# Counting the filling steps of an attention loop from what was really taken, and moving one gate job forward

## The chip, the cores and the metric

The kernel runs on one core of a Trainium2 chip. The core has five engines, each with its own queue of instructions that it works through in order: TensorE (PE; its weight loads are shown as PEld), VectorE (DVE), ScalarE (ACT), GpSimd (POOL) and SyncE (SP, which here only issues transfers). Engines wait for each other through semaphores. The metric is the device time of one execution in microseconds, the median of several runs.

## The reference

One layer of a hybrid encoder on 1024 tokens of width 1024, in float32: a normalised input goes into a wide projection; stick-breaking attention (8 heads of 64) and a gated linear recurrence (4 heads of 128) run on parts of it; their outputs are merged by gates, projected, and followed by a squared-ReLU MLP. Cut to the part around the change:

```python
xn = rmsnorm(x, norm1_g[layer])
u = xn @ w_in[layer].astype(f32)
q_sb, k_sb, v_sb, f_raw, i_hg, q_hg, g_hg, gate_sb, gate_hg = jnp.split(u, list(c), axis=-1)
...
# attention, for each head and each block of 128 queries
z = jnp.einsum('bhqd,bhkd->bhqk', qi, k) * scale
mask = kpos[None, :] < qpos[:, None]
log_beta = jax.nn.log_sigmoid(z)
log_rem = jnp.where(mask, log_beta - z, 0.0)
between = lax.cumsum(log_rem, axis=3, reverse=True) - log_rem
w = jnp.where(mask, jnp.exp(log_beta + between), 0.0)
out = jnp.einsum('bhqk,bhkd->bhqd', w, v)
...
o_hg = merge_heads(o_hg) * jax.nn.silu(g_hg)
merged = g_a * (o_sb @ w_o_sb) + g_b * (o_hg @ w_o_hg)
```

## The kernel before, in words

Every float32 product is made from a high and a low part, so one projection of 128 columns for 512 tokens takes 24 matmuls of 512 columns (`three`, eight times), and two such halves make a job.

Attention runs over 64 items, 8 heads times 8 query blocks, each head's blocks in the order 7, 0, 6, 1, 5, 2, 4, 3. Block b has (b+1)*128 keys. An item passes through four functions. `scores` (line 767) makes the scores `z` on PE and two sigmoids of them on ACT, `rm` and `bt`, and sets one column of `bt` on POOL. `weights` (798) runs the scan over `rm` and multiplies `bt` by it, both on DVE. `turn` (824) transposes `bt` on PE into `pw` and splits that into a high part on ACT (`wTh`) and a low part on DVE (`wTl`). `values` (867) multiplies two finished blocks with V on PE into `po`, and ACT and DVE bring the result into `osb`. The loop at the end of the kernel prepares items ahead: in turn i it calls `weights` for item i+1 and `scores` for item i+2, and then `turn` for item i.

Between these calls it advances a list of other matmul work, `Stream` (487). A job in it is a generator; `step` runs one piece of it, which is six matmuls for a projection. `advance(n, upto)` runs n steps, `finish(upto)` all steps up to a job. The jobs were put in at lines 1458 to 1467: the first job (head 0's queries and keys, and all of V, 45 steps), then queries and keys of heads 1 to 4, then the recurrence's `q_job(0)` and the gate job `raw_job(KT)`, then heads 5 to 7, `f_job(0)`, `f_job(1)`, `q_job(1)`, `f_job(2)`, and `raw_job(KT + 1)`, whose number is `j_att`. A job for queries and keys, f or q has 9 steps, a raw job 8; the last step of each only closes it. `KT` is 8, so the tiles of the two raw jobs are called `wga8`, `pga`, `pgq` and `wga9`: they make the two plain output gates of the recurrence (`g_hg`) together with a partial product that later gates reuse. When a job starts, its weights are split into high and low parts (`wqk2h`, `wqk2l`) and those of the next two jobs are split or loaded, out of a pool with two raw buffers.

The end of a half of a queries-and-keys job (`qk_epilogue`, 664) copies high parts on ACT (`KS`, `QH`), takes low parts on DVE (`KS`, `QL`), and copies Q's two parts into the other 64 partitions by two transfers issued on POOL.

Which order an engine's instructions get is set by the scheduler that builds the kernel, with two lanes for PE: "main" (attention) and "fill" (the stream); a block of filling may not run ahead of the main lane by more than `AHEAD` = 2 blocks.

The loop's budget before:

```python
n_fill = 9 * (NHS - 1 + 5) + 7 + 7 + 4
n_first = 4
...
st.finish(j_qk[items[min(i + 4, len(items) - 1)][0]])
...
want = n_first + (i + 1) * (n_fill - n_first) // len(items)
st.advance(want - done, j_att)
done = want
```

`finish` makes sure that a head's queries and keys are there before its scores. Behind the loop `st.finish(j_att)` runs whatever is left, and the recurrence's stages go on from there.

Of the kernel before, what the change touches and what calls it, by code (L numbers as in the profile page):

```python
# [23 lines left out]
KT = D // P  # L24
# [15 lines left out]
def kernel(  # L40
# [34 lines left out]
    def slot(name, dt=F32):  # L75
        return spool.tile([P, 1024], dt, tag="s", name=name)
# [7 lines left out]
    def bank(name):  # L84
        return psum.tile([P, 512], F32, tag="p", name=name)
# [10 lines left out]
    class Lane:  # L96
        def __init__(self):
            self.ends = []
            self.last = None
            self.gates = ()  # L100
# [9 lines left out]
    def open_block(name):  # L110
        cur[0] = name
        lane = lanes[name]
        lane.gates = (lane.last,)
        if name == "main":
            lane.ends.append(lane.last)
        else:
            ends = lanes["main"].ends
            lane.gates += tuple(ends[-AHEAD : len(ends) - AHEAD + 1])
# [16 lines left out]
    def load(dst, src):  # L135
        last_load[0] = after(nc.sync.dma_start(dst, src), last_load[0])
# [342 lines left out]
    def cols_unit(name, parts):  # L479

        dmas, c = [], 0
        for mat, c0, n in parts:
            dmas.append((c, n, mat[:, c0 : c0 + n].rearrange("(k p) c -> p k c", p=P)))
            c += n
        return Unit(name, [dmas])

    class Stream:
        def __init__(self, eager=False):
            self.eager = eager
            self.jobs = []  # L490
            self.pos = 0
            self.gen = None
            self.steps = 0
            self.owed_t = None

        def add(self, units, body):
            self.jobs.append((units, body))
            return len(self.jobs)
# [25 lines left out]
        def step(self):  # L524

            if self.gen is None:
                if self.pos >= len(self.jobs):
                    return False
                self.steps = 0
                self._start()  # L530
            self.steps += 1
            if self.owed_t and self.steps == 6:
                self.owed_t.split_t(hg_level[0] or turn_lo[0])
                self.owed_t = None
            open_block("fill")
            if next(self.gen, StopIteration) is StopIteration:
                self.gen = None
                self.pos += 1
            return True
# [11 lines left out]
    st = Stream()  # L551

    def three(ps, wh, wl, xh, xl, first, last, goes_on=False):
        matmul(ps, wh, xh, start=first, stop=False, skip_group_check=goes_on)
        matmul(ps, wh, xl, start=False, stop=False, skip_group_check=goes_on)
        matmul(ps, wl, xh, start=False, stop=last, skip_group_check=goes_on)

    def proj_half(ps, hl, mov, nk, half, wcol=lambda k: k * P, ts=slice(0, 512)):
        wh, wl = hl
        for kt in range(nk):  # L560
            c = wcol(kt)
            xh, xl = (t[:, ts] for t in mov(kt, half))
            three(ps, wh[:, c : c + P], wl[:, c : c + P], xh, xl, kt == 0, kt == nk - 1)
            if kt % 2 == 1:
                yield

    def proj_jobs(group, acts):


        def body():  # L570
            for half in range(2):
                for name, unit, ep in group:
                    ps = bank(f"{name}_{half}")
                    yield from proj_half(ps, unit.hl[0], acts.mov, KT, half)
                    ep(ps, half)

        return st.add([u for _, u, _ in group], body)
# [86 lines left out]
    def qk_epilogue(h):  # L664
        def ep(ps, half):
            if half == 0:
                qk[h] = tuple(slot(f"{n}{h}", F32R) for n in ("QH", "QL", "KS"))
            QH, QL, KS = qk[h]
            cs = slice(half * 512, (half + 1) * 512)
            hi_copy(KS[0:64, cs], ps[64:128])  # L670
            hi_copy(QH[0:64, cs], ps[0:64])
            lo_sub(KS[64:128, cs], ps[64:128], KS[0:64, cs])
            last_lo[0] = lo_sub(QL[0:64, cs], ps[0:64], QH[0:64, cs])
            for Q in (QH, QL):
                nc.gpsimd.dma_start(Q[64:128, cs].bitcast(F32), Q[0:64, cs].bitcast(F32))

        return ep

    def qk_item(h):
        u = cols_unit(f"wqk{h}", [(W_IN, C_Q + h * DHS, DHS), (W_IN, C_K + h * DHS, DHS)])  # L680
        return f"pjqk{h}", u, qk_epilogue(h)
# [78 lines left out]
    j_qk = {0: j_first}  # L760

    QB_ORDER = (7, 0, 6, 1, 5, 2, 4, 3)
    items = [(h, qb) for h in range(NHS) for qb in QB_ORDER]
# [472 lines left out]
    def half(name, dt=F32):  # L1236
        return hpool.tile([P, 512], dt, tag="h", name=name)
# [36 lines left out]
    def gate_bias(which, cb):  # L1274
        return prm[:, BG + which * KT + cb : BG + which * KT + cb + 1]
# [44 lines left out]
    def raw_job(cb):  # L1320
        u = raw_units[cb]

        def steps_of(ps, wt, w0, half_, k0, start):
            wh, wl = u.hl[wt]
            for k in range(4):
                c = (w0 + k) * P
                xh, xl = xn.mov(k0 + k, half_)
                three(
                    ps, wh[:, c : c + P], wl[:, c : c + P], xh, xl, start and k == 0, k == 3, True
                )  # L1330
                if k % 2 == 1:
                    yield

        def body():
            p1, p14, g1 = (half(f"{n}_{cb}") for n in ("p1", "p14", "g1"))
            ps, p4 = bank(f"pga{cb}"), bank(f"pgq{cb}")
            if 6 <= cb < KT:
                load_g1(cb - 6)
            if 5 <= cb < KT:
                sb_units[cb - 5].load()  # L1340
            if 3 <= cb < KT - 1:
                osb[cb - 3] = slot(f"osr{cb}")
                load(osb[cb - 3], od[cb - 3])
            yield from steps_of(ps, 0, 0, 0, 0, True)
            hi_behind[0] = nc.scalar.copy(p1, ps)
            nc.scalar.dma_start(pd[cb][:, 0, :], p1)
            u.split_t()
            st.prefetch()
            hi_behind[0] = None
            yield from steps_of(p4, 1, 0, 1, 4, True)  # L1350
            add(p14, p1, p4)
            if cb == 3 or cb == KT - 1:
                whole_input(1, int(cb == KT - 1))
            nc.gpsimd.dma_start(pd[cb][:, 1, :], p14)
            yield from steps_of(ps, 0, 4, 0, 4, False)
            if cb < KT:
                nc.scalar.activation(g1, ps, AF.Sigmoid, bias=gate_bias(0, cb))
            else:
                nc.scalar.activation(g1, ps, AF.Sigmoid)
                mul(g1, ps, g1)  # L1360
            nc.scalar.dma_start(gd[cb], g1)
            if 4 <= cb < KT:
                a_sb.put(cb - 4, osb.pop(cb - 4))

        return st.add([u], body)
# [3 lines left out]
    def load_g1(cb):  # L1369
        g1r[cb] = half(f"g1r{cb}")  # L1370
        load(g1r[cb], gd[cb])
# [4 lines left out]
    def whole_input(i, j):  # L1376
        for kp in range(2):
            h, l = (t.bitcast(F32) for t in xn.t[i, 2 * j + kp])
            nc.gpsimd.dma_start(l, h, accum_op=ALU.add)
            whole[i, j, kp] = l  # L1380
# [76 lines left out]

    for h in range(1, NHS):
        j_qk[h] = proj_jobs([qk_item(h)], xn)
        if h == 4:  # L1460
            q_job(0)
            raw_job(KT)
    f_job(0)
    f_job(1)
    q_job(1)
# [1 line left out]
    j_att = raw_job(KT + 1)  # L1467
# [827 lines left out]
    scores(*items[1])  # L2295

    n_fill = 9 * (NHS - 1 + 5) + 7 + 7 + 4
    n_first = 4
    ready = deque()
    wsums = out_weight_sums()  # L2300
    done = 0
    for i, it in enumerate(items):
        if i + 1 < len(items):
            weights(*items[i + 1])
        if i + 2 < len(items):
            st.finish(j_qk[items[min(i + 4, len(items) - 1)][0]])
            scores(*items[i + 2])
        if i % 2 == 1:
            next(wsums, None)
        want = n_first + (i + 1) * (n_fill - n_first) // len(items)  # L2310
        st.advance(want - done, j_att)
        done = want
        before = ready.popleft() if ready else None

        def between():
            if before:
                values(*before)

        r = turn(*it, between)
        if i == len(items) - 2:  # L2320
            attended[0] = turn_lo[0]
        if it[1] != NT - 1:
            between()
        if r:
            ready.append(r)
# [128 lines left out]
```

## Time and profile before

| | us |
|---|---|
| median of 3 runs | 1438.32 |
| lowest and highest run | 1438.10, 1438.45 |
| profiled execution, its own time | 1437.93 |
| its span from first to last instruction | 1436.2 |
| attention's stretch in it (first 1024-wide scan to last score) | about 60 to 322 |

Times in the trace count from the span's first instruction. A row of the timeline has the start, the duration, the engine, the line, the operation, the output and inputs by the program's tile names, the shape and the count; what stands in brackets behind it is idle time of the engine just before, and what released it. A row of the grouped view has the count, then busy time and the mean in nanoseconds, then idle time ahead of the group. Durations of PE rows overlap, so the distance between two starts tells what a matmul costs in a stream.

### The profile page before, as it was taken

How to read it: one execution, taken by the hardware profiler on the slowest of the kernel's cores; microseconds unless marked ns; L12 is line 12 of the kernel's file. 1: busy time of each engine (PE TensorE's matmuls, PEld its weight loads, DVE VectorE, ACT ScalarE, POOL GpSimd, SP SyncE). 2: the span in 40 equal slices, each digit the busy share in tenths (PEclk: the TensorE clock that was granted, in tenths of full speed). 3: DMA queues.
4: the chain of work that ended last, by engine and by line, in shares of the span. 5: the costliest groups of instructions: out<-in, count | busy, mean ns of one | idle time of the engine just before them, and what ended most of it. 6: DMA issues, size and time to landing. Idle time of an engine off the chain costs nothing.

```text
span 1436.2 us, 19231 instructions
## 1 busy us (share of the span) xinstructions
PE 1423.2 (99%) x7056; PEld 1193.2 (83%) x7056; DVE 1118.6 (78%) x1537; ACT 678.0 (47%) x1177; POOL 146.6 (10%) x338
## 2 busy tenths in 40 slices
PE   9999999999999999999999999999999999999998
PEld 7888888888888888888888888888888888888886
DVE  6579999899677898798788898666666758668765
ACT  6366666664233444333244674444444433524343
POOL 3012222110001031000000300000000000000042
PEclk9999999999999999999999999999999999999999
DMA  7123435434015775545477405444446974776725
GB/s 237 29 66 89 114 88 107 74 82 130 17 45 155 234 190 194 163 160 187 147 272 249 176 30 198 139 138 144 159 154 215 348 268 158 265 275 251 275 101 181
DMA packets 161334, 233.54 MB, mean 163 GB/s; under 512 B 26028, under 2 KB 93144, under 8 KB 161240
## 3 DMA queue, kind: packets, MB, share of 16 engines
q1 hardware_dynamic: 145400, 190.11, 39.3%
q0 software_dynamic: 11520, 34.61, 9.6%
q10 hardware_dynamic: 4320, 7.60, 1.4%
q8 instruction: 55, 0.90, 0.3%
q14 instruction: 39, 0.32, 0.1%
HBM read 167.27 MB, written 65.01 MB: 162 GB/s over the span
## 4 chain that ended last, share of the span: by engine, by line
PE 76%; DVE 0%; POOL 0%; ACT 0%; issue 0%
PE pm L128 21%; PE pX L128 9%; PE pW L128 6%; PE pY L128 6%; PE gX L128 4%; PE gY L128 4%; PE pys L128 3%; PE pga L128 3%; PE pji L128 3%; PE pyh L128 3%; PE sl L128 3%; PE pwX L128 2%; PE pjq L128 2%; PE pgq L128 2%; PE pwY L128 2%; PE pwW L128 2%
## 5 line engine op out<-in xcount | busy, mean ns | idle before, releaser
L156 ACT CAST whid<-w 128x1024 fp32r<-128x1024 f32 x30 | 31.6, 1054 | 154.1 <-PE pm L128 89.6
L808 DVE TENSOR_TENSOR_SCAN rm<-rm,bits 128x511 f32<-128x511 f32 (+7 forms) x72 | 87.0, 1217 | 8.8 <-ACT rm L786 8.4
L128 PE MATMUL pm<-wlod,sh 128*128 128x512 f32 x240 | 93.5, 390 | 0.0
L128 PE MATMUL pm<-whid,sl 128*128 128x512 f32 x240 | 93.4, 389 | 0.0
L128 PE MATMUL pm<-whid,sh 128*128 128x512 f32 x240 | 93.4, 389 | 0.0
L128 PE MATMUL pm<-tl,sh 128*128 128x512 f32 (+1 forms) x210 | 81.3, 387 | 0.0
L128 PE MATMUL pm<-th,sl 128*128 128x512 f32 (+1 forms) x210 | 81.3, 387 | 0.0
L128 PE MATMUL pm<-th,sh 128*128 128x512 f32 (+1 forms) x210 | 81.3, 387 | 0.0
L161 DVE TENSOR_TENSOR wlod<-w,whid 128x1024 fp32r<-128x1024 f32 x30 | 36.6, 1222 | 51.8 <-ACT whid L156 51.8
L161 DVE TENSOR_TENSOR sl<-sa,sh 128x1024 fp32r<-128x1024 f32 x56 | 68.2, 1217 | 0.0
L156 ACT CAST wTh<-pw 128x512 fp32r<-128x512 f32 (+2 forms) x96 | 43.7, 486 | 42.0 <-PE pw L131 36.0
L2090 POOL TENSOR_SCALAR fss<-fss 128x1 f32<-128x1 f32 x8 | 4.5, 560 | 562.1 <-ACT fsc L2085 561.5
L156 ACT CAST sh<-sa 128x1024 fp32r<-128x1024 f32 x56 | 57.2, 1046 | 6.6 <-DMA sa<-ad 6.6
L161 DVE TENSOR_TENSOR wTl<-pw,wTh 128x512 fp32r<-128x512 f32 (+2 forms) x96 | 50.2, 546 | 5.1 <-ACT wTh L156 4.9
L128 PEld LDWEIGHTS pm<-wlod,sh 128*128 128x128 f32 x240 | 45.0, 188 | 9.9 <-DVE wlod L161 0.4
L128 PEld LDWEIGHTS pm<-whid,sl 128*128 128x128 f32 x240 | 45.1, 188 | 9.4
L128 PEld LDWEIGHTS pm<-whid,sh 128*128 128x128 f32 x240 | 45.0, 187 | 9.3
L169 DVE TENSOR_TENSOR bt<-bt,rm 128x511 f32<-128x511 f32 (+7 forms) x72 | 48.7, 684 | 3.7
L128 PE MATMUL pX<-sql,t1h 128*128 128x512 f32 x128 | 50.0, 391 | 0.1
L789 ACT ACTIVATE bt<-z 128x512 f32<-128x512 f32 (+3 forms) x96 | 48.0, 502 | 4.0 <-DMA od<-osb 2.6
L128 PE MATMUL pX<-sqh,t1h 128*128 128x512 f32 x128 | 49.8, 389 | 0.0
L128 PE MATMUL pX<-sqh,t1l 128*128 128x512 f32 x128 | 49.8, 389 | 0.0
(933 smaller groups left out, 4468.1 us busy)
## 6 DMA issues: line engine op xcount, KB each, us to landing
w<-in_w_ff_dram SPq DMA_DIRECT2D x72, 512.0 KB, 6.1
sa<-ad SPq DMA_DIRECT2D x56, 512.0 KB, 7.1
ad<-a SPq DMA_DIRECT2D x32, 256.0 KB, 2.4
ad<-s SPq DMA_DIRECT2D x16, 512.0 KB, 5.7
tw<-in_w_out_dram POOLq DMA_DIRECT2D x24, 256.0 KB, 4.1
pr<-pd SPq DMA_DIRECT2D x10, 512.0 KB, 5.6
x<-in_x_dram SPq DMA_DIRECT2D x8, 512.0 KB, 9.7
xnl<-xnh POOLq DMA_DIRECT2D x8, 512.0 KB, 8.4
```

The lines of the kernel that those rows point to most:

```text
L128: return pe(nc.tensor.matmul(*a, **k))
L156: hi_last[0] = after(in_turn("act", nc.scalar.copy(dst, src)), hi_behind[0])
L161: nc.vector.tensor_tensor(out=dst, in0=src, in1=hi.bitcast(F32), op=ALU.subtract),
L169: return nc.vector.tensor_tensor(out=out, in0=a, in1=b, op=ALU.mult)
L789: nc.scalar.activation(bt[:, s0 : s0 + e], z[:, :e], AF.Sigmoid, scale=0.125)
L808: sc = nc.vector.tensor_tensor_scan(out=rr, data0=rr, data1=bits[:, 1024 - nk + a : 1024 - nk + b][:, ::-1], initial=rm[:, b : b + 1] if i ...
L2090: nc.gpsimd.tensor_scalar(out=ssq, in0=ssq, scalar1=1.0 / D, scalar2=EPS, op0=ALU.mult, op1=ALU.add)
```

## The change

It counts every step the stream takes (`taken`), and sets the budget of a turn against that count, from the count at the loop's start; the constant 4 is gone. Steps run by `finish` are thus part of the budget. `raw_job(KT)` moves from behind head 4's job and `q_job(0)` to behind head 2's job. A `finish(j_qk[0])` is added at turn 2.

```diff
@@ Stream
             self.steps = 0
+            self.taken = 0
             self.owed_t = None
...
             self.steps += 1
+            self.taken += 1
...
     for h in range(1, NHS):
         j_qk[h] = proj_jobs([qk_item(h)], xn)
+        if h == 2:
+            raw_job(KT)
         if h == 4:
             q_job(0)
-            raw_job(KT)
...
     n_fill = 9 * (NHS - 1 + 5) + 7 + 7 + 4
-    n_first = 4
+    taken = st.taken
     ready = deque()
     wsums = out_weight_sums()
-    done = 0
     for i, it in enumerate(items):
...
-        want = n_first + (i + 1) * (n_fill - n_first) // len(items)
-        st.advance(want - done, j_att)
-        done = want
+        if i == 2:
+            st.finish(j_qk[0])
+        st.advance(taken + (i + 1) * n_fill // len(items) - st.taken, j_att)
         before = ready.popleft() if ready else None
```

## The prediction

> **What bounds the kernel now.** I read the page's busy shares first, then who waited for whom on PE, then stage windows, then the order of instructions of both built versions against the timeline. One profiled execution took 1437.93 us, of which its instructions span 1436.2; the median of the runs shown is 1438.32, 0.4 above it.
>
> ```profile
> span 1436.2 us, 19231 instructions
> PE 1423.2 (99%) x7056; PEld 1193.2 (83%) x7056; DVE 1118.6 (78%) x1537; ACT 678.0 (47%) x1177; POOL 146.6 (10%) x338
> ```
>
> PE is idle for 13.0 us of the whole span (1436.2 - 1423.2). PE's own waits show how little of that attention owns:
>
> ```profile
> PE warm L128 <- POOL ident masks.py:199: 2.2, 1, 2.2
> PE pw L131 <- DVE bt L169: 2.2, 2, 1.2
> ```
>
> Attention costs PE two waits for a product on DVE, 2.2 us together: 1.2 at 164 us and 1.0 in its last turns. The reader should see that the matmuls are the bound, that the change neither adds nor removes one, and that the end can therefore move only by what it does to PE's idle time. A gain is limited to about 2.2 us, a loss is not. The windows show why a loss is possible:
>
> ```profile
> 60.00:80.00 20.00, 20.00 (x91) 16.61 (x90) 9.73 (x14) 4.96 (x14) 0.00 (x0) 1.00 0.00 1
> 120.00:140.00 20.00, 20.00 (x115) 17.24 (x113) 19.40 (x28) 13.96 (x32) 5.48 (x20) 1.00 0.39 95
> ```
>
> (columns: length, then busy time of PE, PEld, DVE, ACT, POOL). In mid-attention DVE is busy 19.40 of 20 us: filling and attention are balanced, and PE is full only because projection matmuls stand between attention's turns.
>
> **What the change moves.** Three edits: the counting, the place of the first plain gate job (`wga8`), and a `finish` at turn 2. The last does nothing: at turn 0 the existing `finish` already asks for `j_qk[0]`. Where the gate job stands decides which matmuls fill, not how many; its loads go earlier on SP's queue, ahead of the third head's weights, and are wanted some 30 us after the second raw buffer comes free, so I cost it at nothing (if that cover fails, the job's matmuls wait for a 512 KB load).
>
> The counting is what matters. 36 steps are taken ahead of the loop, and the first job has 45, so `finish` takes 9 in turn 0. Before, these 9 were not counted and turn 0 gave 5 more steps; the steps due after turn i were 4 + (i+1)*122/64 beside them. Afterwards the 9 count: due are (i+1)*126/64, that is 1, 3, 5, 7 in turns 0 to 3, so nothing is filled there. At turn 4 `finish` for the second head takes its whole job (9 steps, 48 matmuls, sum 18), which is again ahead of what is due until turn 9. The same happens, smaller, at turns 12 (4 steps at once, sum 27) and 20 (5 at once, sum 44); from turn 22 on the pace is as before, 9 steps behind. These 9 are made up after the loop. The built orders agree. Up to the score matmul of the second head's second smallest block (I call it M1, at 114.19 us before) the old order has 114 projection matmuls behind 74.01 us, the new one 48. At the same place one head later the lag is 60, later 48.
>
> **The main term, the first head.** These rows of PE and DVE carry it (start, duration):
>
> ```profile
> 73.21 0.39 PE L128 MATMUL z<-KS,QH 128*128 128x512 f32 x1
> 74.01 0.40 PE L128 MATMUL pjqk<-xnh,wqk1h 128*128 128x512 f32 x1
> 80.60 0.39 PE L128 MATMUL pjqk<-xnh,wqk1l 128*128 128x512 f32 x1
> 80.83 1.03 PE L131 MATMUL pw<-ident,bt 128*128 128x128 f32 x8
> 81.94 0.39 PE L128 MATMUL pjqk<-xnh,wqk1h 128*128 128x512 f32 x1
> 84.69 0.27 PE L131 MATMUL pw<-ident,bt 128*128 128x128 f32 x1
> 85.50 0.40 PE L128 MATMUL pjqk<-xnh,wqk1h 128*128 128x512 f32 x1
> 86.87 0.93 PE L131 MATMUL pw<-ident,bt 128*128 128x128 f32 x7
> 87.98 0.39 PE L128 MATMUL pjqk<-xnh,wqk2h 128*128 128x512 f32 x1
> 113.24 0.28 PE L128 MATMUL po<-wTl,V 128*128 128x256 f32 x1
> 113.84 0.60 PE L131 MATMUL pw<-ident,bt 128*128 128x128 f32 x4
> 114.19 0.36 PE L128 MATMUL z<-KS,QH 128*128 128x256 f32 x1
> ...
> 75.64 2.02 DVE L808 TENSOR_TENSOR_SCAN rm<-rm,bits 128x895 f32<-128x895 f32 x1 [0.46 <-ACT rm L786]
> ```
>
> ```profile
> L161 DVE TENSOR_TENSOR wTl<-pw,wTh 128x512 fp32r<-128x512 f32 x48 | 32.4, 678 | 4.4 <-ACT wTh L156 4.2
> L808 DVE TENSOR_TENSOR_SCAN rm<-rm,bits 128x511 f32<-128x511 f32 x16 | 19.4, 1215 | 2.9 <-ACT rm L786 2.7
> L808 DVE TENSOR_TENSOR_SCAN rm<-rm,bits 128x767 f32<-128x767 f32 x8 | 14.0, 1748 | 1.4 <-ACT rm L786 1.3
> L887 DVE TENSOR_TENSOR osb<-po,ot 64x256 f32<-64x256 f32 x32 | 13.4, 418 | 2.0 <-ACT ot L886 1.4
> L808 DVE TENSOR_TENSOR_SCAN rm<-rm,bits 128x639 f32<-128x639 f32 x8 | 11.8, 1481 | 1.6 <-ACT rm L786 1.5
> L169 DVE TENSOR_TENSOR bt<-bt,rm 128x511 f32<-128x511 f32 x16 | 11.0, 690 | 1.4
> L161 DVE TENSOR_TENSOR KS<-pjqk,KS 64x512 fp32r<-64x512 f32 x14 | 9.7, 695 | 4.0 <-ACT QH L156 3.7
> L161 DVE TENSOR_TENSOR QL<-pjqk,QH 64x512 fp32r<-64x512 f32 x14 | 9.5, 681 | 0.2
> L161 DVE TENSOR_TENSOR wTl<-pw,wTh 128x384 fp32r<-128x384 f32 x16 | 8.7, 546 | 0.1
> L169 DVE TENSOR_TENSOR bt<-bt,rm 128x895 f32<-128x895 f32 x8 | 8.7, 1086 | 0.4
> L161 DVE TENSOR_TENSOR wTl<-pw,wTh 128x256 fp32r<-128x256 f32 x16 | 6.6, 413 | 0.0
> L169 DVE TENSOR_TENSOR bt<-bt,rm 128x639 f32<-128x639 f32 x8 | 6.6, 823 | 0.6
> L808 DVE TENSOR_TENSOR_SCAN rm<-rm,bits 128x255 f32<-128x255 f32 x8 | 5.4, 673 | 0.0
> L161 DVE TENSOR_TENSOR wTl<-pw,wTh 128x128 fp32r<-128x128 f32 x16 | 4.5, 279 | 0.7 <-ACT wTh L156 0.7
> L169 DVE TENSOR_TENSOR bt<-bt,rm 128x255 f32<-128x255 f32 x8 | 3.4, 424 | 0.5
> ```
>
> A projection matmul costs PE (80.60 - 74.01)/29 = 0.227 us from start to start. Without idle time M1 would come 66 x 0.227 = 15.0 us earlier, at 99.2. Now DVE's queue in the new order, from the long scan at 75.64, which stays where it is:
>
> - PE: eight transposes and a score (80.83 to 81.94, 1.11) and the next turn's (84.69 to 85.50, 0.81) follow at 74.01 at once and end at 75.9. The next transposes want the 895 product: scan to 77.7, two `wTl` of 512 (1.36), product (1.09): 80.1. Gap 4.2.
> - These seven transposes and a score (86.87 to 87.98, 1.11) end at 81.2; the 255 product comes after 0.28 + 0.67 + 1.75 + 0.42 = 3.1, at 83.2. Gap 2.0.
> - `wTl` 512 and 384 (1.22) end at 84.4, sixteen value products at 0.12 (113.24 to 113.84 is five) end at 86.3, with 2 projection matmuls already among the waiting; 46 more take 10.4: 96.7. PE is full, but DVE has little to do meanwhile.
> - ACT's two copies of the last half (0.58 each, row below) and DVE's two `lo` parts (1.38) follow: 99.3. Only now comes the scan of 639 and behind it DVE's queue up to the `wTl` of the 639 block: 1.48 + 0.68 + 0.41 + 0.42 + 0.82 + 0.55 + 2 x (1.22 + 0.69) + 0.68 + 0.28 = 9.1: 108.4.
> - Then PE: twelve value products (1.4), four score matmuls (0.8, from 73.21 to 74.01), four transposes, eight value products, four transposes (0.35 + 0.96 + 0.35): M1 at 112.3.
>
> Term: 112.3 - 99.2 = **13.1 us of new idle time**. Bounds: if DVE never idled behind 75.64, what I left out between (`bt` 767, `wTl` 256, scan and product of 383, an `osb`, the projection's four `lo` parts and a weight split) included, the same queue ends near 100.8 and M1 comes at 104.7, 5.5 over; if every hop between engines costs 0.15 us more on the ten hops of the chain, 14.6.
>
> **The second and third heads.** Their jobs now end in a burst of 18 matmuls just ahead of the head's first 1024-wide scores, which need the copies of Q into the other partitions. Those are issued on POOL behind a memset of the 639 block's last column.
>
> ```profile
> L156 ACT CAST KS<-pjqk 64x512 fp32r<-64x512 f32 x14 | 8.2, 584 | 4.8 <-PE pjqk L128 4.0 <-issue 0.5
> L786 ACT ACTIVATE rm<-z 128x320 f32<-128x320 f32 x8 | 3.6, 444 | 0.0
> QL<-QL POOLq DMA_DIRECT2D x15, 128.0 KB, 2.2
> 164.06 0.52 PE L131 MATMUL pw<-ident,bt 128*128 128x128 f32 x3 [1.21 <-DVE bt L169]
> ```
>
> ACT's copies (1.2), its four 320-wide sigmoids (1.8), the memset and the copy's landing (2.2): 5.3 us behind the burst. PE has scores, transposes and four value products for about 2.4 of it (estimate, at the spacings above). Gap 2.9 each, bounds 0 (the copy is issued as soon as ACT is through) and 5.3. In the third head the old gap of 1.2 at 164.06 falls away, so 1.7 there.
>
> **The tail.** The 9 late steps stand where PE waited 1.0 for the last products: -1.0, bounds -1.0 and 0. Made-up matmuls themselves cost nothing extra, since the total is unchanged.
>
> Sum: 1437.93 + 13.1 + 2.9 + 1.7 - 1.0 = 1454.6; as a median of runs 1455.
>
> **Rivals.**
>
> The clock falls in the gaps. In the first head PE would work about 1 us of the 7 before the burst. No row here has such a gap in mid-run; the nearest is the start:
>
> ```profile
> 2.25 4.03 PE L128 MATMUL warm<-ident 128*128 128x128 f32 x20 [2.25 <-POOL ident masks.py:199]
> ```
>
> If a restart ran at half pace for as long as this block, it would lose 2.0 us, and one or two restarts fall in front of matmuls that count: +2 to +4, 1457 to 1459. The Trainium skill ("TensorE: Matmul & The Clock Gate", section "HAM oscillation") says that PE gaps over about 3.4 us bring half rate; by its window an estimate of 1.7 us a restart, 1456.7 for one. No run here shows it.
>
> DVE is the only bound: M1 at 104.7, no wait for Q's copies, both old gaps gone: 5.5 - 2.2 = +3.3, 1441. For it: DVE's queue alone is no longer. Against it: the burst at turn 4 stands in front of the scores that feed DVE, in the built order.
>
> Faster: the pace before left PE waiting twice, and the late steps now stand in the last turns, while the third head's gate job covers the first wait: -2.2, 1436. It decides only if the first head's new gap is under 2.2, that is M1 before 101.4; even DVE's queue alone gives 104.7.
>
> That the change does nothing (the `finish` calls forcing the old order) is excluded for the order, and left a small chance for the time: 1438.
>
> **How the numbers follow.** Forecast 0.60, clock 0.15, DVE alone 0.14, nothing 0.05, faster 0.06. The likeliest time is 1455; its own range, from the bounds of the first head's upper end, the copies and the tail, is 1448 to 1461. 1441 to 1463 takes in DVE alone and the clock, and leaves out some 2 in 10. A measurement of this kernel tells about 0.2% (2.9 us) from no change: faster 0.06, same 0.04, slower 0.90.
>
> **What would show it.** In the profile after: PE idle time by some 17 us more, nearly all before 150 us; two gaps of about 4 and 2 us behind 75.9, with `pw` waiting for `bt`; DVE idle during a 46-matmul run of `pjqk`; M1 near 112; waits of `z` for Q's copies ahead of heads 1, 2 and 3; none in the last turns. It is wrong if M1 comes before 105, if matmuls behind the gaps run at over 0.25 us apart, or if the stages behind attention shift among themselves.

## The result, and the profile after

| | before | after |
|---|---|---|
| median of 5 runs each, us | 1438.29 | 1460.48 |
| lowest and highest run, us | 1437.94, 1438.45 | 1459.85, 1462.08 |
| ratio of times, 95% interval | | 1.0157 [1.0142, 1.0172] |
| profiled execution, us | 1437.93 | 1460.48 |

The change makes the kernel 22.2 us slower. These are the page's lines of the span, of PE and of the granted clock in 40 slices (tenths):

```profile
span 1458.6 us, 19228 instructions
PE 1432.4 (98%) x7056; PEld 1201.2 (82%) x7056; DVE 1119.4 (77%) x1537; ACT 678.2 (46%) x1177; POOL 145.8 (10%) x338
...
PEclk9988999999999999999999999999999999999999
```

The same 7056 matmuls are busy for 9.2 us longer than before (1432.4 against 1423.2), and PE is idle for 26.2 us instead of 13.0 (1458.6 - 1432.4). So PE has 13.2 us more with nothing to do, and is busy 9.2 us longer with the same work. The second figure is not yet what the slower work costs, since some of it stands where PE would have waited anyway; e5_warm below tells the two apart. The clock line says where PE is slow: the two slices with an 8 cover 73 to 146 us (36.5 us each).

PE's waits between 60 and 400 us, the view that showed two waits before (what waited, for whom; total, times, longest):

```profile
PE z L128 <- DMA QH<-QH: 7.4, 3, 3.2
PE pw L131 <- DVE bt L169: 4.9, 3, 3.9
...
PE sd L128 <- ACT sd_h L156: 0.8, 1, 0.8
PE sd L128 <- DVE sd_l L161: 0.7, 1, 0.7
```

The largest is new: scores (`z`) that wait for the copies of Q. Transposes (`pw`) wait for DVE's products, value products (`po`) for DVE's low parts, and `sd` are sums of the recurrence behind attention. The windows of the changed kernel (length, busy PE, PEld, DVE, ACT, POOL, granted clock, DMA share, GB/s):

```profile
80.00:90.00 10.00, 9.54 (x43) 8.38 (x44) 6.78 (x11) 2.68 (x6) 0.00 (x0) 0.69 0.00 0
90.00:100.00 10.00, 10.00 (x53) 8.39 (x51) 2.86 (x4) 3.72 (x7) 1.21 (x4) 1.00 0.13 28
100.00:110.00 10.00, 5.23 (x19) 3.88 (x19) 9.73 (x15) 7.18 (x18) 3.67 (x15) 0.66 0.36 106
...
130.00:140.00 10.00, 6.78 (x33) 5.61 (x32) 7.93 (x11) 5.34 (x13) 2.89 (x12) 0.87 0.73 171
```

Read the second and third row together: first PE is full and DVE has 2.86 us of work in ten, then DVE is full (9.73) and PE is half idle. PE runs filling and attention one after the other where it ran them beside each other before.

PE's timeline where the first gap ends:

```profile
80.07 1.73 PE L131 MATMUL pw<-ident,bt 128*128 128x128 f32 x7 [3.90 <-DVE bt L169]
...
82.82 0.66 PE L131 MATMUL pw<-ident,bt 128*128 128x128 f32 x2 [0.39 <-DVE bt L169]
...
83.50 0.63 PE L128 MATMUL pjqk<-xnh,wqk1h 128*128 128x512 f32 x1
83.92 0.63 PE L128 MATMUL pjqk<-xnl,wqk1h 128*128 128x512 f32 x1
84.35 0.41 PE L128 MATMUL po<-wTl,V 128*128 128x256 f32 x1
84.56 0.41 PE L128 MATMUL po<-wTh,V 128*128 128x256 f32 x1
...
86.23 0.28 PE L128 MATMUL po<-wTh,V 128*128 128x256 f32 x1
86.34 0.28 PE L128 MATMUL po<-wTl,V 128*128 128x256 f32 x1
```

The gap of 3.90 is the one predicted as 4.2. Behind it the distance between starts is 0.42 for a projection matmul and 0.21 for a value matmul; from 86.23 on it is 0.11 to 0.12 again. The second predicted gap (2.0) shrank to 0.39: the transposes and scores ahead of it took 2.4 us (80.07 to 82.43) where the prediction had 1.1.

How much time has been lost so far can be read at the second, third and fourth head's score of block 1, the marks: with fewer filling matmuls done, the changed kernel should be there earlier. Rows before (the first mark's is in the prediction), after, and in the run with idle work of the next section (label e5_warm):

```profile
145.12 0.36 PE L128 MATMUL z<-KS,QH 128*128 128x256 f32 x1
...
178.90 0.36 PE L128 MATMUL z<-KS,QH 128*128 128x256 f32 x1
```

```profile
115.26 0.36 PE L128 MATMUL z<-KS,QH 128*128 128x256 f32 x1
...
152.64 0.36 PE L128 MATMUL z<-KS,QH 128*128 128x256 f32 x1
...
187.21 0.36 PE L128 MATMUL z<-KS,QH 128*128 128x256 f32 x1
```

```profile
112.07 0.36 PE L128 MATMUL z<-KS,QH 128*128 128x256 f32 x1
...
148.32 0.36 PE L128 MATMUL z<-KS,QH 128*128 128x256 f32 x1
...
182.89 0.36 PE L128 MATMUL z<-KS,QH 128*128 128x256 f32 x1
```

At these marks the changed kernel has done 66, 60 and 60 filling matmuls fewer than the old one, and 48 fewer at the last score of this kind (counted in the timelines from 74 us on). At 0.227 us each the marks would stand at 99.2, 131.5 and 165.3 without a loss:

| lost up to | predicted | after | with idle work in the gaps |
|---|---|---|---|
| first mark | 13.1 | 16.1 | 12.9 |
| second mark | 16.0 | 21.1 | 16.8 |
| third mark | 17.7 | 21.9 | 17.6 |
| last score of this kind, at 320.77 us | 17.7 | 21.7 | 17.3 |

So all of it is lost by 190 us, and the rest of attention repeats the old pace.

### The profile page after: what moved, and what is told of

It reads as the page before. It is cut to its first block, busy times and chain, and to the rows that moved or that the text cites. A ratio compares the mean times of both kernels' runs of the same rounds, so it can differ in the third digit from the quotient of the medians.

```text
span 1458.6 us, 19228 instructions
## 1 busy us (share of the span) xinstructions
PE 1432.4 (98%) x7056; PEld 1201.2 (82%) x7056; DVE 1119.4 (77%) x1537; ACT 678.2 (46%) x1177; POOL 145.8 (10%) x338
## 4 chain that ended last, share of the span: by engine, by line
PE 93%; DVE 2%; ACT 1%; DMA 1%; issue 1%; POOL 0%; SPq 0%; ACTq 0%; DVEq 0%; POOLq 0%
PE pm L128 21%; PE pX L128 9%; PE pW L128 6%; PE pY L128 6%; PE pjqk L128 5%; PE gX L128 4%; PE gY L128 4%; PE pga L128 3%; PE pys L128 3%; PE pji L128 3%; PE pyh L128 3%; PE pjf L128 3%; PE pjv L128 3%; PE po L128 3%; PE sl L128 2%; PE pjq L128 2%
## 5 line engine op out<-in xcount | busy, mean ns | idle before, releaser
L788 ACT ACTIVATE rm<-z 128x511 f32<-128x511 f32 (+4 forms) x96 | 48.2, 502 | 8.1 <-issue 3.8
L131 PE MATMUL pw<-ident,bt 128*128 128x128 f32 x288 | 45.1, 282 | 4.9 <-DVE bt L169 4.9
```

Source lines behind the costliest of these rows:

```text
L131: return pe(nc.tensor.transpose(dst, src, ident))
L788: nc.scalar.activation(rm[:, s0 + c0 - 1 : s0 + m - 1], z[:, c0:m], AF.Sigmoid, scale=-0.125)
```

## The experiments

Each diff is against the changed kernel, unless it says otherwise.

**The two parts apart.** e1_count leaves the gate job where it was, so only the counting is left. e2_place is the kernel before with nothing but the job moved.

```diff
 e1_count
-        if h == 2:
-            raw_job(KT)
         if h == 4:
             q_job(0)
+            raw_job(KT)

 e2_place, against before
+        if h == 2:
+            raw_job(KT)
         if h == 4:
             q_job(0)
-            raw_job(KT)
```

> The counting alone; the gate job stays behind head 4's job. Theory (starved first turns): the first head's order is the same as with the whole change, so nearly all of the loss stays: 1457 to 1463, PE idle again ahead of the transposes at 75 to 80 us, granted clock about 0.992. Rival (the gate job's place costs it): under 1442.

> The gate job's place alone, with the old counting. In the built order this is the same kernel as the changed one with 13 steps put on top of the budget (9 of the first job and the old constant 4). Theory: nothing to starve, 1436 to 1440, clock 0.999. Rival (the place costs it): 1450 or more.

Measured: e1_count 1454.93 us (1454.53 to 1455.95), 1.0120 [1.0105, 1.0135] of before, 2 us under the range expected; e2_place 1437.55 (1437.09 to 1438.07), 0.9998 [0.9988, 1.0007]. PE's two largest waits of e1_count in total:

```profile
PE pw L131 <- DVE bt L169: 5.4, 2, 3.9
PE z L128 <- DMA QH<-QH: 4.4, 2, 2.2
```

The counting alone loses 17.0 us (1454.93 - 1437.96). The place alone costs nothing that can be measured; it trades the wait of 1.2 at 164 us for three short ones, 1.1 together. Yet the two together lose 22.2, some 5 more than the counting alone. The prediction had put the place itself at nothing; what the 5 us are made of is taken up with e9_behind3.

**How much of the pace is missing.** e3_lead6 gives six steps ahead and takes two of them back by the end. With 13 steps ahead and the end as before (9 from `finish` and the old constant 4), the counting gives every turn the same number of steps as e2_place, so that kernel is the other end of the scale.

```diff
-        st.advance(taken + (i + 1) * n_fill // len(items) - st.taken, j_att)
+        st.advance(taken + 6 + (i + 1) * (n_fill - 2) // len(items) - st.taken, j_att)
```

> The whole change with 6 steps put on top of the budget at the start (4 of them still there at the end), about half of the 13 that the old counting was ahead. Theory (gaps, and a clock that falls only behind the long ones): less than half of the loss is left, 1440 to 1447, clock 0.997 or more. Rival (the loss is in proportion to the missing steps): half of 22, 1448 to 1451.

Measured: 1442.87 (1441.91 to 1443.91), 1.0029 [1.0017, 1.0041]. With a budget that starts 13, 7 and 0 steps under the old one, the kernel loses 22.2, 4.5 and nothing. The loss is far from proportional: PE's longest wait is 2.2 us here, and the granted clock is 0.998 over the run, against 0.992 after.

**What the slow matmuls cost.** e5_warm puts 59 small matmuls of the identity, whose product nothing reads, where the changed kernel's PE waits: ahead of the transposes in turns 2, 3, 6 and 7, and ahead of the scores in turns 6, 14 and 22. It adds work and takes none away; only the clock can gain by it.

```diff
+    IDLE_TURN = {2: 16, 3: 6, 6: 3, 7: 6}
+    IDLE_SCORES = {6: 9, 14: 12, 22: 7}
+    def idle_work(n):
+        open_block("main")
+        spare = bank("spare")
+        for _ in range(n):
+            matmul(spare[:, 0:P], ident, ident, start=True, stop=True)
...
+            if i in IDLE_SCORES:
+                idle_work(IDLE_SCORES[i])
...
+        if i in IDLE_TURN:
+            idle_work(IDLE_TURN[i])
```

> The whole change, with 59 matmuls of the identity on itself, whose results nobody reads, put into PE's gaps: 16 and 6 ahead of the third and fourth turn, 9, 12 and 7 ahead of the first 1024-wide scores of heads 1 to 3, 3 and 6 ahead of turns 6 and 7. They add work and take no wait away. Theory with two parts (idle time, and matmuls at a lower clock behind the gaps): the clock goes back to 0.998 or more and the time falls by 4 to 7 us, to 1453 to 1457. Rival (idle time alone; the lower clock lies under waits for DVE anyway): 1459 to 1463.

Measured: 1455.70 (1455.18 to 1456.71), 1.0125 [1.011, 1.014]. Two windows of it, where the changed kernel had a granted clock of 0.91 and 0.89:

```profile
60.00:100.00 40.00, 39.25 (x226) 34.05 (x225) 21.65 (x33) 15.38 (x39) 2.63 (x9) 1.00 0.06 16
100.00:160.00 60.00, 56.93 (x351) 49.88 (x350) 54.64 (x77) 37.59 (x87) 11.78 (x47) 1.00 0.39 107
```

The clock stays at 1.00, and the loss against before falls from 22.2 to 17.7 us. The clock's part is therefore at least 4.5 us. What is left was lost at full clock: it is lack of work for PE, and the table of marks shows 12.9, 16.8 and 17.6 here.

**What the forced steps do.** e4_guard does not call the first head's `finish` ahead of the scores, so the first job's steps come by the count, the last of them by the `finish` at turn 2.

```diff
-            st.finish(j_qk[items[min(i + 4, len(items) - 1)][0]])
+            if items[min(i + 4, len(items) - 1)][0] > 0:
+                st.finish(j_qk[items[min(i + 4, len(items) - 1)][0]])
```

> The whole change, but the finish ahead of the scores is not called for head 0, so the 9 steps left of the first job (48 matmuls of V) are paced by the budget too and the new finish at turn 2 does something. Theory: the gaps ahead of the third and fourth turn (4 and 2 us) are filled, the later ones of the first two heads stay: 1450 to 1456. Rival (what matters is how many steps the loop lags at its end, not where they are missing): 1459 to 1462, as with the whole change.

Measured: 1452.74 (1452.01 to 1452.86), 1.0102 [1.0087, 1.0117]: 7.4 us of 22.2 come back. PE is full from 60 to 90 us, and both early gaps are gone. But the burst for the second head still stands in one piece, up to 90.4 us, and what follows it stays:

```profile
PE z L128 <- DMA QH<-QH: 4.2, 2, 2.1
PE z L128 <- ACT bt L791: 2.7, 1, 2.7
```

**Bursts two turns earlier.** If only the lack of work before a burst mattered, asking for a head's queries and keys two turns earlier should fill the first gap and let Q's copies land in time. e6_ahead6:

```diff
-            st.finish(j_qk[items[min(i + 4, len(items) - 1)][0]])
+            st.finish(j_qk[items[min(i + 6, len(items) - 1)][0]])
```

> The whole change, with the finish ahead of the scores looking six items ahead instead of four, so that each head's burst of queries and keys comes two turns earlier (turns 2, 10 and 18). The number of steps behind, at the end of the first head and of the loop, stays. Theory (what costs is where the missing steps leave PE without work, and that the copies of Q come too late behind a burst): the 48 matmuls of head 1 fall into the first gap, PE no longer waits for Q's copies in any head: 1444 to 1453. Rival (a lag of 9 to 13 steps costs its PE time wherever it stands): 1457 to 1462.

Measured: 1464.10 (1462.13 to 1465.16), 1.0173 [1.0156, 1.019]: slower still, above both ranges expected. The first gap is filled and no score waits for Q's copies. DVE's timeline and PE's waits show what came in their place:

```profile
87.46 1.23 DVE L161 TENSOR_TENSOR wga8wlo<-wga8r,wga8whi 128x1024 fp32r<-128x1024 f32 x1 [3.74 <-ACT wga8whi L156]
```

```profile
PE po L128 <- DVE wTl L161: 5.5, 5, 1.3
PE po L128 <- ACT wTh L156: 7.5, 4, 2.1
```

The unbroken block of 48 projection matmuls now runs ahead of a score that feeds DVE. DVE sits idle for 3.74 us in it, and when the block is over, PE waits for ACT and DVE (13.0 us in nine waits of `po`). In both places where it was tried the block hurts: while it runs DVE starves, and behind it PE does. Up to the third mark the kernel has lost as much as the full change (its third mark stands at 187.1); a further burst for head 5 near 221 us, with waits of 2.1 and 1.3, brings the rest.

**The gate job one head later.** e9_behind3 puts it behind head 3's job.

```diff
-        if h == 2:
+        if h == 3:
             raw_job(KT)
```

> The whole change, but the gate job behind head 3's job instead of head 2's. Theory (with the late pace the gate job's 8 steps ahead of head 3's queries and keys force a third burst at turn 20, and its weight work stands in front of the copies of Q): both go, as with the counting alone: 1453 to 1457, two waits for Q's copies instead of three. Rival (an early gate job costs by itself): 1458 to 1462.

Measured: 1457.32 (1455.59 to 1458.26), 1.0129 [1.0114, 1.0144]: 18.9 above its own before, between e1_count (17.0) and the full change (22.2), and just above what was expected. Its waits for Q's copies are two of 2.2, as in e1_count. The issues of transfers in the window of the second wait (130 to 140 us) tell the two apart; first after, then e1_count (size, time from issue to landing):

```profile
wqk4r<-in_w_in_dram SPq DMA_DIRECT2D x2, 256.0 KB, 4.1
...
QH<-QH POOLq DMA_DIRECT2D x1, 128.0 KB, 4.1
```

```profile
QH<-QH POOLq DMA_DIRECT2D x1, 128.0 KB, 2.1
```

With the gate job behind head 2, the following heads' weights are loaded just while Q's copy is under way: it takes 4.1 us instead of 2.1, and the wait grows to 3.22. In e4_guard, e5_warm and e9_behind3 too a copy of Q beside the loads of `wqk4r` took 3.6, 3.8 and 3.6 us. That the loads are the cause is read from the times alone: a copy at 124.70 us in the changed kernel took 3.2 us with no such load under way. And the full change has a third burst, at turn 20, with a wait of 2.0, which the other two do not have. Both together are 3.0 us (7.4 - 4.4), and 3.3 us lie between e9_behind3 and the full change (22.2 - 18.9). The two profiles differ by 3.9: 0.9 of it stands at the first mark already, 0.8 comes in the second head and 2.3 in the third, so the fit is near but not a proof. The 2 us between e1_count and e9_behind3 are left open: their profiled spans differ by 0.5 only (1454.2 and 1454.7), and their runs scatter by 1.4 and 2.7.

**Repairing the start.** e7_guard9 has e4_guard's edit and gives 9 steps ahead, so that the first turns are filled again; the loop ends five steps behind the old count.

```diff
+            if items[min(i + 4, len(items) - 1)][0] > 0:
...
+        st.advance(taken + 9 + (i + 1) * (n_fill - 5) // len(items) - st.taken, j_att)
```

> The whole change with two repairs: the finish ahead of the scores isn't called for head 0 (so the first job's last 9 steps are paced), and 9 steps stand on top of the budget at the start, 4 at the end. Every step is counted as the change means it, but in the built order there is filling in every turn but one of the first two heads, and the loop ends 5 steps behind the old count. Theory (evenness decides, not the count): 1435 to 1440, clock 0.999, no PE wait over 1 us but the one for Q's copies. Rival (a lag at the end costs its PE time): 5 steps of 1.4 us, 1444 to 1446.

Measured: 1441.12 (1439.62 to 1441.79), 1.0019 [1.001, 1.0028], about 1 above the range. PE is full from 60 to 100 us. A single turn of the second head has no filling matmul, as its one step only closes a job, and the first matmul of the next job (`pga`) waits for DVE's `wTl`:

```profile
114.07 0.50 PE L128 MATMUL pga<-xnh,wga8whi 128*128 128x512 f32 x1 [2.62 <-DVE wTl L161]
...
115.10 0.43 PE L128 MATMUL pga<-xnl,wga8whi 128*128 128x512 f32 x1
115.33 0.62 PE L128 MATMUL pga<-xnh,wga8wlo 128*128 128x512 f32 x1
115.75 0.63 PE L128 MATMUL pga<-xnh,wga8whi 128*128 128x512 f32 x1
```

2.62 us of waiting, and 1.3 us after it has ended the distance goes from 0.23 to 0.42.

**The late steps alone.** In the tail I had counted a gain of 1.0 for steps left over behind the loop. e8_tail is e2_place with a budget that is five steps smaller at its end. The old budget has used up all steps by turn 61 (turns run from 0 to 63); with this one matmuls are left for the last turns.

```diff
 e8_tail, against e2_place
-        want = n_first + (i + 1) * (n_fill - n_first) // len(items)
+        want = n_first + (i + 1) * (n_fill - n_first - 5) // len(items)
```

> The old counting and the gate job's new place, with the budget of the loop 5 steps smaller at its end, so that 5 steps are left for the last turns. Theory (late steps cover PE's wait of about 1 us for the last products): that wait goes, 1436 to 1437.5, 0 to 1.5 under the gate job's place alone. Rival (the late steps push the next stage's first sums behind DVE, as the waits for sd_l and sd_h with the whole change suggest): 1438 to 1440.

Measured: 1442.41 (1440.72 to 1442.71), 1.0025 [1.0015, 1.0034], 4.2 above its own before, where e2_place stood 0.4 below: above the expected range and above the rival's. PE's waits, 60 to 400 us:

```profile
PE po L128 <- DVE wTl L161: 3.4, 4, 2.0
PE sd L128 <- ACT sd_h L156: 0.8, 1, 0.8
PE sd L128 <- DVE sd_l L161: 0.3, 1, 0.3
```

The wait for the last products is indeed gone. In its place the recurrence's sums (`sd`) wait 1.1 us at 339 us for parts that ACT and DVE have not made yet, and the slightly thinner filling opens a wait of 2.0 in mid-attention, with a granted clock of 0.97 from 100 to 160 us. At its last score of the kind used as marks e8_tail is already 5.0 us behind e2_place (24 fewer filling matmuls counted), of 5.3 between the two spans. So nearly all of its loss lies in mid-attention, and in the tail the trade is about even.

No version run here is measurably faster than the kernel before.

## Why the prediction came out as it did

Predicted were 1455 and a range of 1441 to 1463; measured were 1460.48. The forecast's mechanism is the one that happened, with the clock's rival on top of it. The likeliest time missed by 5.5 us; the range holds the result because it was drawn to take in the clock.

- *The counting as the cause*: right. Alone it loses 17.0 us, and with fewer steps missing the loss falls, faster than in proportion (e3_lead6).
- *First head, 13.1*: the idle part was right, and the size was off. The gap of 4.2 measured 3.90; DVE went idle in the burst, as said; the mark came at 115.26 instead of 112.3. With the clock held up by idle work it came at 112.07, 12.9 us late. The 3.2 us between went when the clock was held, and are put down to it.
- *Second head, 2.9*: measured 5.0 (21.1 - 16.1), and 3.9 with the clock held. The waits for Q's copies came ahead of heads 1, 2 and 3, as said, but not by the way given: the memset on POOL that I put ahead of the copies ran before the burst had ended. Ahead of the first of them ACT has a split of the next job's weights. Its rows, and those of POOL and PE:

```profile
97.41 1.05 ACT L156 CAST wga8whi<-wga8r 128x1024 fp32r<-128x1024 f32 x1 [4.08 <-issue]
...
99.08 0.58 ACT L156 CAST QH<-pjqk 64x512 fp32r<-64x512 f32 x1
```

```profile
99.96 0.52 POOL L677 DMA_DIRECT2D QH<-QH  x1 [4.01 <-ACT QH L156]
```

```profile
102.24 0.71 PE L128 MATMUL z<-KS,QH 128*128 128x512 f32 x2 [2.18 <-DMA QH<-QH]
```

  The copy is issued 0.3 us after ACT has made `QH`, and PE goes on 2.3 us later, 4.8 us behind the burst's end at 97.4, where 5.3 was predicted. The split took the place of the sigmoids in the sum, so the size was near. In the second head no split stands ahead, and the wait of 3.22 comes from the transfer itself (next point).
- *The moved loads cost nothing*: wrong. I looked for the gate job's matmuls waiting for their load. The loads instead met Q's copy, which took 4.1 us instead of 2.1 (as said above, by the times alone).
- *Third head, 1.7*: measured 0.8 (21.9 - 21.1): a new wait of 2.04, and the old one of 1.2 gone.
- *Tail, -1.0*: wrong in sign. The profiled time is 22.55 above before and the loss at the third mark 21.9, so what follows cost about 0.6; the wait for the last products went, and 1.5 us for `sd` came. e8_tail shows the same trade by itself.
- *Counts of steps*: three were off, and no term hangs on them. The gate job has 7 steps, not 8 (its 36 matmuls and a closing step), so turn 20 forces 4 and not 5. From turn 22 the lag is 11 steps, and 9 only late in the loop. And of these 9 only 5 are left behind the loop, since the old budget has used up its steps by turn 61.
- *The clock as a rival, 2 to 4 us instead of nothing*: it came true together with the forecast, and larger. The price was one or two restarts; the clock fell in the first head's two idle stretches and again in the second head (0.69, 0.66 and 0.87 in the windows), in finer windows to half from 79.3 to 86.2, 103.2 to 113.5 and 137.4 to 140.8 us. At least 4.5 us are its share. The sign that the prediction named against itself, matmuls behind a gap over 0.25 us apart, is there: 0.42. So the step that failed in the forecast is the clock, put at nothing.
- *DVE alone, nothing, faster*: excluded. No stage behind attention moved against the others: from 340 us on each starts 22.4 or 22.5 us later than before.

The sum by the runs: 17.6 us of missing work up to the third mark (predicted 17.7), 4.3 of clock (21.9 - 17.6; predicted nothing), 0.6 in the tail (predicted -1.0), together 22.5. That the missing work comes so near is partly luck: the second head was put too low by 1.0 (2.9 against 3.9) and the third too high by 0.9 (1.7 against 0.8).

What stays open: which part of the 22.2 us would remain if Q's copies landed at once (no kernel separates this from the burst), and the 2 us between e1_count and e9_behind3.

## What to carry to other kernels

When filler work is paced by a budget, count the steps that a dependency forces apart from the paced ones: forced steps charged to the budget come out as a burst, and the turns behind or ahead of it get nothing. What counts is the evenness: the same 7056 matmuls took 1438 to 1464 us, and putting the block earlier only changed which engine starved first. A gap on PE can cost more than its length, so price one of 2 us or more with the slow stretch that may follow it.

## What was unexpected in the hardware

The clock falls after shorter gaps than I had thought, and late. Besides the 3.90 us above, 2.62 us in e7_guard9 halved the pace, and so did 2.01 us in e8_tail, from 0.8 us after its end (125.49) until 128.9 us:

```profile
124.67 0.38 PE L128 MATMUL po<-wTl,V 128*128 128x256 f32 x1 [2.01 <-DVE wTl L161]
```

while a gap of 2.04 us in the changed kernel did not:

```profile
172.71 0.70 PE L128 MATMUL z<-KS,QH 128*128 128x512 f32 x2 [2.04 <-DMA QH<-QH]
```

So the length of one gap does not decide it here. What does can be read from windows. In every trace the stretches between two changes of the granted clock are whole multiples of 3.41 us, so a run can be cut into windows of that length with the changes at their edges. Columns as above; first e8_tail, then the changed kernel, then e4_guard:

```profile
122.08:125.49 3.41, 1.34 (x10) 1.01 (x9) 3.41 (x5) 2.04 (x6) 0.70 (x4) 1.00 0.88 273
125.49:128.90 3.41, 3.41 (x17) 3.31 (x16) 2.22 (x5) 1.10 (x4) 0.00 (x0) 0.50 0.79 197
```

```profile
168.08:171.49 3.41, 2.59 (x20) 2.21 (x18) 1.33 (x3) 3.40 (x8) 0.52 (x1) 1.00 0.02 4
171.49:174.91 3.42, 2.20 (x10) 1.88 (x11) 3.42 (x7) 2.50 (x7) 2.37 (x11) 1.00 0.61 149
```

```profile
162.99:166.40 3.41, 1.67 (x7) 1.44 (x8) 3.41 (x6) 3.00 (x8) 2.37 (x11) 1.00 0.50 119
166.40:169.81 3.41, 3.41 (x20) 2.88 (x19) 3.41 (x5) 2.76 (x7) 0.00 (x0) 1.00 0.31 112
```

The gap of e8_tail lies in one window, PE is idle for 2.07 us of it (3.41 - 1.34), and the next window runs at half the clock: the change comes at the edge, and so some time after the gap. The gap of the changed kernel is cut by an edge into windows with 0.82 and 1.22 us idle, and the clock stays. 1.74 us idle in one window of e4_guard have no effect either. From 60 to 400 us the eleven traces have 18 windows at full clock with 1.88 us idle or more, and half the clock follows each of them; it follows none with 1.74 or less. This is read off the traces; no run moved a gap across an edge to test it. The Trainium skill ("TensorE: Matmul & The Clock Gate", section "HAM oscillation") warns of gaps over about 3.4 us; the slow stretch of 3.4 us in e8_tail (125.5 to 128.9) agrees with the length of the window that this page gives, the gap that suffices (2.01 us) does not. The other surprise is the transfer: a copy of 128 KB inside the core took 3.6 to 4.1 us beside weight loads, against 2.1 in e1_count.
